# Adaptive max pooling on one core: from Tile's dependencies to one critical section with semaphores set by hand

## The chip, the core and the metric

The kernel runs on one core of a Trainium2 chip. The metric is the device time of one execution in microseconds (us), here the median of several runs. Beside it there is a profile of one further execution, taken by the hardware profiler: its span goes from the first to the last instruction of the program, and its times are counted from the start of that span.

Four parts of the core matter here. SP (SyncE) issues transfers (DMAs) and waits on semaphores. DVE (VectorE) reduces. ACT (ScalarE) issues one transfer. Sixteen DMA engines move the data for all of them. A transfer that is issued adds 16 to a semaphore when it has landed. "SPq" or "DVEq" in the profile is the part of an engine that handles waits and issues; these aren't counted as busy.

## The reference

The input is 32 x 256 x 4096 float32 (134.2 MB); each row of 4096 is cut into 256 windows, and the output has the maximum of each window (8.4 MB).

```python
for i in range(output_size):
    start = int(i * length / output_size)
    end = int((i + 1) * length / output_size)
    result[:, :, i] = np.max(x[:, :, start:end], axis=-1)
```

4096 / 256 = 16, so all windows are 16 long and don't overlap. In memory the task is a list of 32 x 256 x 256 windows, each of 16 neighbouring numbers.

## The kernel before, in words

**Layout.** The 2,097,152 windows are dealt to 128 partitions, 16384 each, in two groups. In group A each partition has 13436 neighbouring windows, in group B 2948. Every transfer is one contiguous run per partition.

**Loads.** Group A comes in 14 loads of 128, 12 times 1024, and 1020 windows per partition, from the end of the group to its start; group B in three, of 1024, 1024 and 900. That makes 17 loads. One of 1024 windows has 65536 bytes per partition, 8.4 MB in all. All are issued by SP, in the order of the loop: the small first one at L87, the 16 others at L96.

**Ring.** There are two places for loads in the tile `ring`, each 1024 + 152 windows wide. Loads take the two places in turn, and each second load of a place is shifted by 152 windows (`GAP`). DVE reduces a load in two pieces, 872 and 152 windows, and begins with the 872 windows that the next load of this place will overwrite. That next load needs the first piece only. It doesn't touch the other 152 windows.

**Reductions.** `pooled` (L56) is one `reduce_max` over the 16 numbers of each window, from `ring` to the tile `kept`, where all results but those of the last load stay. The last load is reduced in one piece, into the end of its own place in `ring`. There are 32 reductions: 1 + 15 x 2 + 1.

**Stores.** There are three: group A from `kept` (6718 KB), group B's first two loads from `kept` (1024 KB), and the last 900 windows from `ring` (450 KB). The last one is issued by ACT (L114), the other two by SP (L117). `tc.no_sync_barrier()` ahead of them keeps their place in the order of the program: they stand behind all loads in SP's stream and therefore in its DMA queue.

**Who makes the waits.** All of it is written in a Tile context. Tile follows which bytes of which tile each instruction reads and writes, and makes the semaphores and waits: a reduction waits for its load, a load for the landing of the older load in this place and for the first piece of its reduction, a store for its reductions. An instruction carries a wait of its own; where there are more, short EVENT_SEMAPHORE instructions stand ahead of it on the same engine. L134 is the program's opening (constants and a barrier of all engines), L148 the Tile context, to which its closing is put down: waits of SP for the transfers, a barrier of all engines, a clearing of the semaphores, and a second barrier.

Of the kernel before, what the change touches and what calls it, by code (L numbers as in the profile page):

```python
# [1 line left out]

# [4 lines left out]


@with_exitstack
def kernel(  # L10
    ctx: ExitStack,
    tc: tile.TileContext,
    x: bass.AP,
    output_size: bass.AP,
    out: bass.AP,
):

    nc = tc.nc
    P = nc.NUM_PARTITIONS
    fp32 = mybir.dt.float32

    B, C, L = x.shape
    O = int(output_size)  # L30
    assert L % O == 0, (L, O)
    W = L // O
    total = B * C * O // P
    assert B * C * O % P == 0

    CHUNK = 1024
    GAP = 152
    FIRST = 128
    LOADS_A, LOADS_B = 13, 2

    LESS = 4
    group_a = [FIRST] + [CHUNK] * (LOADS_A - 1) + [CHUNK - LESS]
    last = total - sum(group_a) - LOADS_B * CHUNK
    group_b = [CHUNK] * LOADS_B + [last]
    assert 0 < last and last * (W + 1) <= CHUNK * W

    pool = ctx.enter_context(tc.tile_pool(name="pool", bufs=1))
    ring = pool.tile([P, 2 * (CHUNK + GAP) * W], fp32, tag="ring", name="ring")
    kept = pool.tile([P, total - last], fp32, tag="kept", name="kept")

    xw = x.flatten_outer_dims().rearrange("r (o w) -> (r o) w", w=W)
    ow = out.flatten_outer_dims().rearrange("r o -> (r o)")

    def pooled(dst, at, n):

        nc.vector.reduce_max(  # L56
            out=dst,
            in_=ring[:, at * W : (at + n) * W].rearrange("p (n w) -> p n w", w=W),
            axis=mybir.AxisListType.X,
        )  # L60

    taken = 0

    def group(n):

        nonlocal taken
        span = slice(taken * P, (taken + n) * P)
        taken += n
        return (
            xw[span].rearrange("(p n) w -> p (n w)", p=P),  # L70
            ow[span].rearrange("(p n) -> p n", p=P),
        )

    stores = []
    n_loads = 0
    base = 0
    for g, loads in enumerate((group_a, group_b)):
        xg, og = group(sum(loads))
        a = sum(loads) if g == 0 else 0
        for n in loads:  # L80
            if g == 0:
                a -= n
            xn = xg[:, a * W : (a + n) * W]
            dst = kept[:, base + a : base + a + n] if n != last else None
            if n == FIRST:

                nc.sync.dma_start(  # L87
                    out=ring[:, CHUNK * W : (CHUNK + n) * W], in_=xn
                )
                pooled(dst, CHUNK, n)  # L90
            else:

                low = n_loads % 2 * (CHUNK + GAP)
                moved = n_loads // 2 % 2
                at = low + moved * GAP
                nc.sync.dma_start(out=ring[:, at * W : (at + n) * W], in_=xn)  # L96
                if n != last:
                    cut = CHUNK - GAP if moved else GAP
                    parts = [(0, cut), (cut, n)]
                    for u, v in parts if moved else parts[::-1]:  # L100
                        pooled(dst[:, u:v], at + u, v - u)
                else:
                    end = (at + CHUNK) * W
                    last_kept = ring[:, end - n : end]
                    pooled(last_kept, at, n)
                n_loads += 1
            if g:
                a += n
        full = a - last if g else sum(loads)
        stores.append((og[:, 0:full], kept[:, base : base + full]))  # L110
        base += full
    assert taken == total

    nc.scalar.dma_start(out=og[:, full : full + last], in_=last_kept)  # L114
    tc.no_sync_barrier()
    for dst, src in stores:
        nc.sync.dma_start(out=dst, in_=src)  # L117


# [1 line left out]
_INS = ['x', 'output_size']  # L121
_OUTS = [((32, 256, 256), 'float32')]

_NUMBERS = {'output_size': 256}


# [26 lines left out]
```

## Time and profile before

| what | value |
|---|---|
| median of 3 runs | 335.02 us (335.02 to 335.04) |
| span of the profiled execution | 333.1 us, 113 instructions |
| its own time: span, and what lies around it | 333.1 us, and 335.02 - 333.1 = 1.9 us if it took as long as the median |
| DVE busy | 276.5 us (83%), 32 reductions |
| of these: 872 windows, 14 times | 205.6 us, 14686 ns each |
| 152 windows, 15 times | 40.1 us, 2676 ns each |
| the last 900 windows | 15.1 us |
| moved | 134.22 MB read, 8.39 MB written, 428 GB/s over the span |
| issue to landing: load of 8192 KB | 24.0 us, median of 14 |
| big store, small store (SP) | 37.2 us, 18.1 us |
| last store (ACT) | 4.2 us |

The page's parts used below are: 2, the span in 40 slices with one digit of busy tenths each; 3, the DMA queues (q1 is fed by SP, q10 by ACT) with packets, megabytes, and the share of the 16 engines that they took; 6, the transfers from issue to landing. A timeline row gives start and length in us, engine, line, operation, tiles and shapes, how many instructions were merged in the row, and in brackets how long the engine sat idle before it and what ended that. A row of waits reads: who waited, for whom, us in total, how often, the longest. A transfer's time from issue to landing includes its time in the queue behind others.

### The profile page before, as it was taken

To read this page: it belongs to the slowest core of one execution; us is meant where nothing else is said; L and a number is where in the kernel's file an instruction comes from. 1 tells how busy PE (TensorE), PEld (TensorE's weight loads), DVE (VectorE), ACT (ScalarE), POOL (GpSimd) and SP (SyncE) were. 2 spreads that over 40 slices of the span, in tenths; PEclk is the share of its full clock that TensorE was granted. 3 is DMA by queue.
4 is the path that set the end of the run, shared out by engine and by line. 5 is a ranking of instruction groups with operands and counts; after the bars stand their busy time and mean duration, and the time that the engine had idled before them with its cause. 6 is when DMAs were issued, how large, how long until landed. Compare 5 with 4: busy or idle time off the path is not lost.

```text
span 333.1 us, 113 instructions
## 1 busy us (share of the span) xinstructions
DVE 276.5 (83%) x32; POOL 0.2 (0%) x4
## 2 busy tenths in 40 slices
DVE  2009979797997979799797979979797998979993
POOL 0000000000000000000000000000000000000000
DMA  9898989899898989899898989899898989899996
GB/s 378 378 504 378 504 378 496 386 441 441 378 504 378 504 378 496 386 457 425 378 504 378 504 378 504 378 441 441 385 494 377 504 378 504 378 458 443 421 413 285
DMA packets 2880, 142.61 MB, mean 428 GB/s; under 512 B 320, under 2 KB 320, under 8 KB 448
## 3 DMA queue, kind: packets, MB, share of 16 engines
q1 hardware_dynamic: 2736, 142.15, 98.8%
q10 hardware_dynamic: 144, 0.46, 0.3%
HBM read 134.22 MB, written 8.39 MB: 428 GB/s over the span
## 4 chain that ended last, share of the span: by engine, by line
DMA 57%; DVE 36%; DVEq 5%; issue 0%; SPq 0%
DMA ring<-in_x_dram 57%; DVE kept L56 36%; DVEq L148 5%; SPq L87 0%
## 5 line engine op out<-in xcount | busy, mean ns | idle before, releaser
L56 DVE TENSOR_REDUCE kept<-ring 128x152 f32<-128x2432 f32 (+3 forms) x31 | 261.4, 8472 | 51.5 <-DMA ring<-in_x_dram 51.5
L56 DVE TENSOR_REDUCE ring<-ring 128x900 f32<-128x14400 f32 x1 | 15.1, 15144 | 0.0
L134 POOL MEMSET const-bfloat16-1.0<- 128x1 bf16 x1 | 0.1, 102 | 0.0
L134 POOL MEMSET const-uint8-127<- 128x1 uint8 x1 | 0.1, 102 | 0.0
L134 POOL MEMSET const-float32-0.0<- 128x1 f32 x1 | 0.1, 99 | 0.2 <-issue 0.2
L134 POOL MEMSET const-float32-1.0<- 128x1 f32 x1 | 0.1, 99 | 0.0
## 6 DMA issues: line engine op xcount, KB each, us to landing
ring<-in_x_dram SPq DMA_DIRECT2D x1, 8160.0 KB, 23.9
ring<-in_x_dram SPq DMA_DIRECT2D x1, 7200.0 KB, 21.6
out_dram<-kept SPq DMA_DIRECT2D x1, 6718.0 KB, 37.2
ring<-in_x_dram SPq DMA_DIRECT2D x1, 1024.0 KB, 4.7
out_dram<-kept SPq DMA_DIRECT2D x1, 1024.0 KB, 18.1
out_dram<-ring ACTq DMA_DIRECT2D x1, 450.0 KB, 4.2
ring<-in_x_dram SPq DMA_DIRECT2D x14, 24.0
```

The costliest lines, as they stand in the source:

```text
L56: nc.vector.reduce_max(out=dst, in_=ring[:, at * W : (at + n) * W].rearrange("p (n w) -> p n w", w=W), axis=mybir.AxisListType.X,)
L134: nc = _bacc.Bacc("TRN2", target_bir_lowering=False, num_devices=1)
L148: with _tile.TileContext(nc) as tc:
```

## The change

The loop no longer issues anything. It makes a list, `plan`, with for each load its source, place, size, the load whose first piece it needs, the pieces and where they go. A second loop inside `tc.tile_critical()` issues the same instructions in the same order on the same engines, and every wait is written out: three semaphores for landings, used in turn, one that counts reductions, and one for each store. Inside such a section Tile makes no waits of its own; it treats the section as one unit. Each reduction adds 1 to `pooled`. At the end SP waits for the three stores. The barrier-like `tc.no_sync_barrier()` is gone.

The first loop, cut to its core:

```diff
-                nc.sync.dma_start(
-                    out=ring[:, CHUNK * W : (CHUNK + n) * W], in_=xn
-                )
-                pooled(dst, CHUNK, n)
+                at, moved, needs = CHUNK, 0, None
+                pieces = [(0, n)]
...
+                moved = n_full // 2 % 2
+                at = n_full % 2 * (CHUNK + GAP) + moved * GAP
+                needs = n_full - 2
+                cut = CHUNK - GAP if moved else GAP
+                pieces = [(0, cut), (cut, n)] if moved else [(cut, n), (0, cut)]
+                if n == last:
+                    pieces = [(0, n)]
+                n_full += 1
...
+            plan.append((xn, at, n, needs, pieces, dsts))
...
-    nc.scalar.dma_start(out=og[:, full : full + last], in_=last_kept)
-    tc.no_sync_barrier()
-    for dst, src in stores:
-        nc.sync.dma_start(out=dst, in_=src)
```

The section (`first_piece[k]` is the count of reductions at which the first piece of full load k is done, `all_pieces[i]` the count after all pieces of load i):

```diff
+    with tc.tile_critical():
+        for i, (xn, at, n, needs, pieces, dsts) in enumerate(plan):
+            if needs is not None and needs >= 0:
+                nc.sync.wait_ge(pooled, first_piece[needs])
+            nc.sync.dma_start(
+                out=ring[:, at * W : (at + n) * W], in_=xn
+            ).then_inc(landed[i % 3], 16)
+            nc.vector.wait_ge(landed[i % 3], 16 * (i // 3 + 1))
+            for (u, v), dst in zip(pieces, dsts):
+                nc.vector.reduce_max(
+                    out=dst,
+                    in_=ring[:, (at + u) * W : (at + v) * W].rearrange(
+                        "p (n w) -> p n w", w=W
+                    ),
+                    axis=mybir.AxisListType.X,
+                ).then_inc(pooled, 1)
+        for i, (dst, src) in enumerate(stores[:2]):
+            nc.sync.wait_ge(pooled, all_pieces[len(group_a) - 1 if i == 0 else -2])
+            nc.sync.dma_start(out=dst, in_=src).then_inc(stored[i], 16)
+        nc.scalar.wait_ge(pooled, all_pieces[-1])
+        nc.scalar.dma_start(out=stores[2][0], in_=stores[2][1]).then_inc(stored[2], 16)
+        for sem in stored:
+            nc.sync.wait_ge(sem, 16)
```

More of the change, by code (lines that the diff above doesn't have):

```diff
@@ L52 @@
     ow = out.flatten_outer_dims().rearrange("r o -> (r o)")
[L54 to L59, printed above, removed]
-        )
     taken = 0
@@ L72, in group @@
         )
+    plan = []
     stores = []
-    n_loads = 0
     base = 0
+    n_full = 0
     for g, loads in enumerate((group_a, group_b)):
@@ L83 @@
             xn = xg[:, a * W : (a + n) * W]
-            dst = kept[:, base + a : base + a + n] if n != last else None
             if n == FIRST:
-                nc.sync.dma_start(
-                    out=ring[:, CHUNK * W : (CHUNK + n) * W], in_=xn
-                )
-                pooled(dst, CHUNK, n)
-            else:
[L93 to L102, printed above, removed]
+                at, moved, needs = CHUNK, 0, None
+                pieces = [(0, n)]
+            else:
+                moved = n_full // 2 % 2
[6 more added lines that the diff above has]
+                n_full += 1
+            dsts = []
+            for u, v in pieces:
+                if n == last:
                     end = (at + CHUNK) * W
                     last_kept = ring[:, end - n : end]
-                    pooled(last_kept, at, n)
-                n_loads += 1
+                    dsts.append(last_kept)
+                else:
+                    dsts.append(kept[:, base + a + u : base + a + v])
+            plan.append((xn, at, n, needs, pieces, dsts))
             if g:
@@ L112 @@
     assert taken == total
-    nc.scalar.dma_start(out=og[:, full : full + last], in_=last_kept)
-    tc.no_sync_barrier()
-    for dst, src in stores:
-        nc.sync.dma_start(out=dst, in_=src)
+    stores.append((og[:, full : full + last], last_kept))
+    landed = [nc.alloc_semaphore(f"landed{i}") for i in range(3)]
+    pooled = nc.alloc_semaphore("pooled")
+    stored = [nc.alloc_semaphore(f"stored{i}") for i in range(3)]
+    count, first_piece, all_pieces = 0, [], []
+    for xn, at, n, needs, pieces, dsts in plan:
+        if needs is not None:
+            first_piece.append(count + 1)
+        count += len(pieces)
+        all_pieces.append(count)
+    with tc.tile_critical():
[21 more added lines that the diff above has]
+            nc.sync.wait_ge(sem, 16)
 _INS = ['x', 'output_size']
```

## The prediction

> **What bounds the kernel now.** I read the page from the transfers inwards: first the busy slices and the queues, then the waits, then the two ends.
>
> Part 2 of the page has one digit for each fortieth of the span, and part 3 the share of the 16 transfer engines that each queue took:
>
> ```profile
> DMA  9898989899898989899898989899898989899996
> ...
> q1 hardware_dynamic: 2736, 142.15, 98.8%
> q10 hardware_dynamic: 144, 0.46, 0.3%
> ```
>
> The queue that SP feeds (q1) occupies the 16 engines 98.8% of the whole span. The same view asked for the stretch 5 to 330 us, without the ends, says:
>
> ```profile
> DMA packets 2553, 140.09 MB, mean 431 GB/s; under 512 B 274, under 2 KB 274, under 8 KB 274
> ...
> q1 hardware_dynamic: 2553, 140.09, 99.6%
> ```
>
> So for 325 us there is no idle transfer time to win. The chain of waits seems to say otherwise: it gives DMA 57% and VectorE (DVE) 36%, in turn. The timeline and the waits of SP's queue show why that isn't a bound of DVE:
>
> ```profile
> 24.78 17.28 DVE L56 TENSOR_REDUCE kept<-ring 128x872 f32<-128x13952 f32 x2 [17.04 <-DMA ring<-in_x_dram]
> 39.50 19.68 SPq L96 DMA_DIRECT2D ring<-in_x_dram  x2
> 44.14 17.28 DVE L56 TENSOR_REDUCE kept<-ring 128x872 f32<-128x13952 f32 x2 [2.08 <-DMA ring<-in_x_dram]
> ```
>
> ```profile
> SPq L96 <- DVE kept L56: 205.6, 14, 14.7
> SPq L96 <- DMA ring<-in_x_dram: 78.4, 14, 22.7
> ```
>
> A load lands and DVE starts at 24.78. After its first piece (14.7 us, the wait of SP just above) SP issues the next load at 39.50; but the load issued before it is still moving and lands only at 44.14. The queue therefore holds at least 44.14 - 39.50 = 4.6 us of work whenever a load is issued. The chain follows the buffer that was released last; the queue in front of it is what takes the time. DVE idles about 2.07 us ahead of each load.
>
> At the end the question is whether the last reduction or the transfers are late:
>
> ```profile
> 312.82 15.14 DVE L56 TENSOR_REDUCE ring<-ring 128x900 f32<-128x14400 f32 x1
> 312.94 0.34 SPq L117 DMA_DIRECT2D out_dram<-kept  x1
> 328.00 0.37 ACTq L114 DMA_DIRECT2D out_dram<-ring  x1
> ```
>
> ACT issues the last store at 328.00, and its landing, 4.2 us later (part 6), is the last event of the work. The queue view of 328 to 330.2 us shows that it isn't DVE that sets this:
>
> ```profile
> q1 hardware_dynamic: 115, 0.92, 99.4%
> issues: line engine op xcount, KB each, median us to landing
> out_dram<-ring ACTq DMA_DIRECT2D x1, 450.0 KB, 4.2
> ```
>
> In these 2.2 us no packet of q10, the ACT queue, runs; all 16 engines are still at SP's last store (99.4%). The first load of the kernel shows how soon packets can follow an issue: it is issued at 0.73, and the stretch 0.5 to 1.5 has a DMA share of 0.00, the stretch 1.5 to 2.0 one of 0.94, so 0.8 to 1.3 us. ACT's packets could have run from about 329.0 (at 1.0). They start after 330.2, so ACT and the reduction ahead of it have some 1.2 us of room (0.9 with the longer start).
>
> So **the time is one stream of transfers, from the first issue at 0.73 to the landing at 332.2**, with what stands before and after it. An edit counts only if it moves the first issue, opens a hole in the stream, or changes what follows 332.2.
>
> **The base of the sum.** The profiled span is 333.1 us. The median of the plain runs is 335.02, so 335.02 - 333.1 = 1.9 us lie around the span. No edit touches what lies there, and I carry the 1.9 over.
>
> **The change, part by part.**
>
> Loads. Before each of 14 loads SP waits twice, for an older landing (78.4 us in all) and then for DVE (205.6 us); the new text has only the second wait, with the same piece as its condition. The landing wait always ends first (at 44.1, against a DVE piece that ends at 58.8), so taking it out saves 14 short instructions of 17 to 28 ns that nobody waits for: 0. The cover is the 4.6 us in the queue; without it each later issue would cost its own length.
>
> DVE's waits. They are now instructions ahead of the reductions. Today one such instruction stands on DVE at this line, 21 ns long; others are part of the reduction. 17 of them are 0.4 us of DVE time, at the most 0.1 us each if the reduction behind a wait starts later, 1.7 us, against 2.07 us of idle time ahead of each load. In the middle it costs nothing. At the end, two of them (load 16 and the last) delay the last reduction by 0.04 to 0.2 us, and ACT's own separate wait is 0.04 more (its one wait instruction today takes 38 ns). All of it lies inside the 1.2 us of room: 0. Without that room it would be 0.1 to 0.24 us.
>
> Stores. SP now waits for all of group A before the first store: those pieces end at 256.93 + 17.21 = 274.1, and the store is issued at 291.4, behind the last load. 0. The second store waits for the same piece as today (21.1 us of SP's time, until 312.9), while its queue still holds 6.7 MB of the first store: 0. What is queued behind this wait on SP is only the final waits. The order on q1 (loads, big store, small store) and on q10 stays.
>
> Entering the section. Tile opens and closes a section on all engines together, and the trace of before has no such boundary. Its nearest rows are the barriers of the closing code, as waits of SP on the last engine to arrive:
>
> ```profile
> SPq L148 <- DMA out_dram<-kept: 17.8, 1, 17.8
> SPq L148 <- DMA out_dram<-ring: 1.1, 1, 1.1
> SPq L134 <- PEq L134: 0.7, 1, 0.7
> SPq L148 <- PEq L148: 0.6, 2, 0.4
> ```
>
> The two closing barriers cost SP 0.6 us: 0.2 for the plain one, 0.4 for the one with drains and a clearing of semaphores in it; the opening one 0.7, with four memsets inside. A boundary at the entry stands ahead of the first issue, so its price is the price of the kernel. From below: SP leaves the opening barrier at about 0.66 and issues at 0.73, so no more than 0.07 can be gained. From above: 0.7, as the opening. I take 0.2, the plain barrier, because nothing has to be drained there.
>
> Leaving the section, and the tail. Today SP's wait for ACT's store (the 1.1 us row) ends at 332.2; one more wait of 28 ns and two drains stand before the closing barrier, until 332.4; the span ends at 333.1. In the new text the wait for ACT's store is the last of three, so the wait behind it goes: -0.1. The section's end adds a boundary: 0.2 by the same row. From below: if the section's own end stands in for the closing, at most the 333.1 - 332.2 = 0.9 us after the landing could go. From above: 0.7 again.
>
> The Trainium skill's page "Runtime: NRT & Kernel Launch", section "The ~15µs preamble/postamble breakdown", prices a pass over all five engines at about 355 ns (8 hops of 44). It speaks of the runtime's barrier, not of Tile's, and against this change: by it two boundaries would be 0.7 us, an estimate, and the kernel would come to 335.6. The trace's 0.2 decides for the sum above.
>
> Sum: 333.1 + 0.2 (entry) + 0.2 (exit) - 0.1 (wait) = 333.4 us of span, and 333.4 + 1.9 = **335.3 us**, 0.1% over before. Its own range is 335.0 to 335.6, each boundary between nothing and 0.35.
>
> **The rivals.**
>
> Slower: heavy boundaries. Each end of the section costs not a plain barrier but one with drains, 0.4 us, up to the 0.7 of the opening. For it: leaving a section has to make sure that every engine is done, as the closing code has. Against: at both places the engines have nothing left to do. 333.1 + 0.8 to 1.4 - 0.1 + 1.9 = 335.7 to 336.3. It is slower by over 0.2% (0.67 us) from 0.39 us for a boundary on. Chance 0.20.
>
> Faster: a shorter closing. Since all work lies in the section, the closing has no semaphores of loads and reductions to look after, and the barrier with the clearing (0.4) or nearly everything after the landing (0.9) falls away: 334.6 to 334.1. For it: four wait instructions of SP stand there for eight semaphores that Tile made itself. Against: three of the four are over before 332.2, and the barriers come with the Tile context, which stays. It decides from 0.67 us, three quarters of that stretch. Chance 0.12.
>
> Not what it says: Tile's closing waits stay as they are, and the three waits stand ahead of them; then nothing goes and 335.4 is the time, not to be told from no change. Chance 0.10.
>
> Slower by a hole: a hand-set count releases a load over 4.6 us late, each time, and the queue runs dry. Each further us then counts 14 times: from 0.05 us past that room on it decides (14 x 0.05 = 0.7), and with 0.1 it gives 335.3 + 1.4 = 336.7. Against: the counts name the same pieces as today. Chance 0.03.
>
> **How the numbers follow.** My forecast has 0.55. Within 0.2% of before, about what a measurement of this kernel can tell from no change, lie the forecast and the closing that stays: 0.65. Faster by more: 0.12. Slower by more: 0.20 + 0.03 = 0.23. The range is 334.6 to 336.2: it leaves out the shorter closing (0.12), the hole (0.03) and the dearest end of the heavy boundaries (some 0.04).
>
> **What would show it.** In the profile after, q1 should again hold 98 to 99% of the span, and loads should land 19.3 to 19.4 us apart. The first issue should come at 0.9 instead of 0.73, the last landing at 332.4, and 0.9 to 1.0 us should follow it. If the first issue stays at 0.73, there is no barrier at the entry. If more than 1.6 us follow the landing, the heavy boundaries are right; if less than 0.5, the shorter closing. The forecast is wrong in its ground if a zero appears among the DMA digits, or if ACT's packets start at once after its issue: then the last reduction counts, and the waits on DVE with it.

## The result, and the profile after

| | before | after |
|---|---|---|
| median of 21 runs each | 335.09 us (334.92 to 335.37) | 335.66 us (335.52 to 335.82) |
| ratio, 95% interval | | 1.0017 (1.0012 to 1.0023) |
| span of the profiled execution | 333.1 us | 334.0 us |

The changed kernel takes 0.57 us (0.17%) longer. 335.3 was forecast, 0.28 us over before; the sign is right and the size about half.

The stream of transfers is as it was. The page's queue rows of the profile after:

```profile
DMA  9898989989898989899898989899998989899996
...
q1 hardware_dynamic: 2736, 142.15, 98.6%
q10 hardware_dynamic: 144, 0.46, 0.3%
```

The two waits ahead of a load have become one, and the sum is about the same: 284.8 us where there were 205.6 + 78.4 = 284.0. Here are SP's waits after:

```profile
SPq L127 <- DVE kept L132: 284.8, 14, 37.6
SPq L141 <- DVE kept L132: 21.1, 1, 21.1
SPq L145 <- DMA out_dram<-ring: 18.9, 1, 18.9
...
SPq L176 <- PEq L176: 0.5, 2, 0.3
```

The loss stands at the two ends. The chain in order of time (start, length, what) begins like this, first before, then after:

```profile
0.66 0.07 issue
0.73 0.37 SPq L87
```

```profile
0.71 0.01 SPq L123
0.72 0.06 issue
0.78 0.03 SPq L176
0.81 0.12 issue
0.94 0.38 SPq L127
```

L123 is the section, L176 the Tile context. SP sends a signal, waits for its own signal in a branch (DVE and ACT do so too, PE and POOL have no such instruction), and 0.12 us pass until the first issue after the branch. The first load is issued at 0.94 instead of 0.73: 0.21 us.

The other end is the code of the section after the last landing, in the view of one line from 332.7 us on (engine, operation, count, shortest, median and longest duration in ns, first and last start):

```profile
L123 SPq EVENT_SEMAPHORE  x2: 17/22/28, 333.0 to 333.2; - x2
L123 SPq COMPARE_BRANCH  x1: 33/33/33, 332.8 to 332.8; - x1
L123 ACTq DRAIN  x1: 8/8/8, 333.0 to 333.0; - x1
L123 DVEq DRAIN  x1: 10/10/10, 333.0 to 333.0; - x1
L123 SPq DRAIN  x1: 7/7/7, 333.1 to 333.1; - x1
L123 SPq NOP  x1: 13/13/13, 333.2 to 333.2; - x1
```

ACT's store is issued at 328.55 and lands 4.2 us later, at 332.73 by the trace. Then come a branch, a signal to three engines, a drain on each, and SP's waits for the answers; only at 333.3 does the closing of the Tile context begin. No instruction here lasts over 33 ns; the time passes between them, behind SP's branch, as at the entry, and in the handing over between engines. From the last landing to the end of the span it is 333.97 - 332.73 = 1.24 us, before it was 333.06 - 332.20 = 0.86: 0.38 us. In e4, e8 and e5 below, which have the same end, it is 1.24, 1.24 and 1.22 us.

0.21 + 0.38 = 0.59 us, against 0.57 measured. The two profiled spans are 0.9 us apart, because the stream between the ends took 331.5 us in one execution and 331.8 in the other. The medians of the spans say that those 0.3 us are the scatter of single executions: they are 333.3 to 333.4 for the kernel before (its runs beside e1, e5 and e9) and 333.9 for the changed one. Less the ends of the profiles, 0.73 + 0.86 and 0.94 + 1.24, both leave a stream of 331.7 to 331.8 us.

### The profile page after: what moved, and what is told of

It reads as the page before. It is cut to its first block, busy times and chain, and to the rows that moved or that the text cites. A ratio compares the mean times of both kernels' runs of the same rounds, so it can differ in the third digit from the quotient of the medians.

```text
span 334.0 us, 105 instructions
## 1 busy us (share of the span) xinstructions
DVE 276.5 (83%) x32; POOL 0.2 (0%) x4
## 3 DMA queue, kind: packets, MB, share of 16 engines
q1 hardware_dynamic: 2736, 142.15, 98.6%
## 4 chain that ended last, share of the span: by engine, by line
DMA 57%; DVE 40%; issue 0%; SPq 0%
DMA ring<-in_x_dram 57%; DVE kept L132 36%; DVE ring L132 5%; SPq L127 0%; SPq L176 0%; SPq L123 0%
```

## The experiments

The theory was that the whole loss is made by the two ends of the section, and that the waits set by hand, the counters and the order of work cost and gain nothing. Its rival was that the hand-set waits slow the stream. Further runs test what the prediction leaned on: the cover of 4.6 us ahead of each load, and the room of ACT's store. "Around the span" is a run's time less its span.

**e1: the same waits, no section.**

```diff
-    nc = tc.nc
+    nc = tc
...
-    pool = ctx.enter_context(tc.tile_pool(name="pool", bufs=1))
-    ring = pool.tile([P, 2 * (CHUNK + GAP) * W], fp32, tag="ring", name="ring")
-    kept = pool.tile([P, total - last], fp32, tag="kept", name="kept")
+    ring = nc.alloc_sbuf_tensor("ring", [P, 2 * (CHUNK + GAP) * W], fp32).ap()
+    kept = nc.alloc_sbuf_tensor("kept", [P, total - last], fp32).ap()
...
-    with tc.tile_critical():
+    if True:
...
-    with _tile.TileContext(nc) as tc:
-        tile_adaptive_max_pool_1d_kernel(tc, *args)
+    tile_adaptive_max_pool_1d_kernel(nc, *args)
```

> The same loads, reductions, stores and hand-set waits as in the changed kernel, but with no section and no Tile context around them: nothing is entered or left, and SP's three waits for the stores are the last instructions. Theory 1 (the section's two ends are the whole loss: 0.21 us at the entry and 0.38 us after the last landing): the first issue is back at 0.73 us, the stream of transfers lasts 331.5 us as before, and with the closing (0.8 us after the landing) gone as well the time is 335.09 - 0.8 = 334.3 us, at least below 334.7. Rival (the waits set by hand slow the stream itself; in the two profiles first issue to last landing is 331.5 us before and 331.8 after): the stream stays at 331.8 and the time is 334.6 us. Second rival (the closing is needed anyway, the runtime's own ending takes its place): 335.1 us, as before.

Measured: 333.94 us, ratio 0.9965 (0.9952 to 0.9977) to before. The chain begins as it did before the change, and behind SP's waits for the stores (L144) no further instruction follows:

```profile
0.73 0.37 SPq L126
```

```profile
L144 SPq EVENT_SEMAPHORE  x2: 17/22/28, 331.4 to 332.6; - x2
```

The first issue is back at 0.73 with all waits set by hand, so the waits don't move it. The time fell by 1.7 us against the changed kernel and is 0.4 us under what the theory said: the medians of the spans are 333.4 and 332.6, so 0.8 us went in the span, as expected, and another 0.4 around it (1.35 instead of 1.8). The second rival's 335.1 is refuted. The time alone doesn't refute the first rival, whose 334.6 didn't reckon with the 0.4 us either, and the profiled run does have a stream of 331.8 us. The median span does: less 0.73 and the 0.05 us behind the landing it leaves 331.8 us, against the 331.7 to 331.8 of before and after. The 331.5 was one short execution. e9 asks where the other 0.4 us went.

**e9: e1 with one barrier at the end.**

```diff
         for sem in stored:
             nc.sync.wait_ge(sem, 16)
+        nc.all_engine_barrier()
```

> The kernel of e1 (no section, no Tile context) with one plain barrier of all engines after SP's waits for the stores. In e1 the span got 0.75 us shorter than before's (332.55 against 333.3, medians of its runs) and what lies around it 0.45 us (1.35 against 1.8). Theory (the second part comes from the engines that end early and do their share of the runtime's ending while SP still waits; a barrier takes that away): span 332.55 + 0.2, around it 1.8, time 334.55 us. Rival (the time around the span is shorter because nothing of Tile is left in the program, barrier or not): 332.75 + 1.35 = 334.1 us.

Measured: 334.59 us (0.9986 of before, 0.9977 to 0.9995), the median of the spans 332.8, so 1.8 us around it. SP's wait in the barrier:

```profile
SPq L145 <- PEq L145: 0.2, 1, 0.2
```

The barrier costs 0.2 us inside the span and 0.45 outside. The rival's 334.1 is refuted, and the time fits the theory: without the barrier, the four other engines come to the end of the program early, and their part of what the runtime does after a kernel no longer stands behind SP's. That it is this part is inferred from the times; the views show no instruction of it. The Trainium skill, page "Runtime: NRT & Kernel Launch", section "The ~15µs preamble/postamble breakdown", lists after a kernel a barrier that waits for all engines, about 1.5 us, and then a reset of some 51 semaphores for each engine, about 1.5 us. No run here shows either; what it is that can be done early stays open, and the runs only put it at 0.45 us. (Against the before measured beside each, e1 gains 1.21 and e9 0.46 us, so the whole barrier is worth 0.65 to 0.75 us.)

**e2: a section in the kernel before.**

```diff
+    idle = nc.alloc_semaphore("idle")
+    with tc.tile_critical():
+        for eng in (nc.vector, nc.scalar, nc.sync):
+            eng.nop().then_inc(idle, 1)
```

> The kernel before with one section ahead of everything, in which DVE, ACT and SP do one empty instruction each; all waits of the loads, reductions and stores are still Tile's. Theory 1 (the ends of a section cost 0.2 us to enter and 0.4 us to leave, and all of it ahead of the first issue counts in full): first issue at 1.3 us instead of 0.73, and 335.09 + 0.6 = 335.7 us. Rival (the loss comes from the waits set by hand): 335.1 us, and the first issue at most 0.2 us later.

Measured: 338.17 us, 3.0 us more than before, which neither theory gives. The chain shows what happened:

```profile
0.79 4.85 DMA ring<-in_x_dram
5.63 0.02 issue
5.65 0.02 SPq L153
...
6.03 0.07 issue
6.10 21.99 DMA ring<-in_x_dram
```

Tile put the first load ahead of the section's work and made the section wait for its landing. The second load is issued at 6.10 instead of 1.15, and from about 5.3 to 7.0 us no transfer runs in the trace. As a price of the ends the run is worthless; it shows what else a section can do in a stream of Tile's instructions.

**e5: the same section ahead of the changed kernel's own,** where no transfer can slip in front.

> The changed kernel with a second section, of one empty instruction each on DVE, ACT and SP, ahead of the first, so that no transfer can slip in between. Theory 1 (entering costs SP 0.2 us, leaving 0.5 us of which 0.1 stood in the closing anyway, and all that lies ahead of the first issue counts): first issue at 0.94 + 0.7 = 1.6 us, time 335.66 + 0.7 = 336.4 us, landing to end as in the changed kernel (1.2 us). Rival (what was lost comes from the hand-set waits in the section, not from its ends): 335.7 us.

Measured: 336.35 us (1.0039 of before, 1.0026 to 1.0052), 0.69 us more than with one section. The chain:

```profile
1.51 0.03 SPq L180
1.55 0.12 issue
1.67 0.38 SPq L131
```

The first issue moved by 1.67 - 0.94 = 0.73 us, and the time by 0.69. The theory held: one section, entered and left, costs 0.7 us, and whatever stands ahead of the first issue counts in full.

**e4 and e8: a later last reduction.** e4 adds the reduction shown, e8 one of 2432 numbers.

```diff
+    spare = pool.tile([P, 40], fp32, tag="spare", name="spare")
...
+            if n == last:
+                back = plan[i - 1][1] * W
+                nc.vector.reduce_max(
+                    out=spare,
+                    in_=ring[:, back : back + 640].rearrange("p (n w) -> p n w", w=16),
+                    axis=mybir.AxisListType.X,
+                )
             nc.vector.wait_ge(landed[i % 3], 16 * (i // 3 + 1))
```

> The changed kernel with one more reduction of 640 numbers per partition ahead of the last one, by the rate of the others (14.69 us for 13952 numbers) 0.7 us; its result is not used. Theory (ACT's store has some 1.1 us of room, since its packets wait for SP's last store): ACT issues 0.7 us later, its packets start at the same time, 335.66 us. Rival (the last reduction sets the end): 336.3 us.

> The changed kernel with one more reduction of 2432 numbers per partition ahead of the last one (2.6 us by the 152-window row), its result unused. Theory (ACT's store has 1.1 us of room): ACT issues at 331.1 instead of 328.5, 2.6 - 1.1 = 1.5 us of it show, 337.2 us, and ACT's packets start about 1 us after the issue. Rival (no room, DVE sets the end): 335.66 + 2.6 = 338.2 us. Rival (ACT's store needs its 2.1 us from issue to the first packet by itself): also 338.2, with the packets 2.1 us after the issue.

Measured: e4 335.65 us, against 335.66 of the changed kernel, though ACT issues at 329.28 instead of 328.55. e8 336.65 us, 0.99 more. The timeline and the stretches of e8 (start and end; share of the transfer engines in the last but one column, then GB/s):

```profile
331.12 0.37 ACTq L152 DMA_DIRECT2D out_dram<-ring  x1
```

```profile
331.00:331.50 0.50, 0.09 (x1) 0.00 (x0) 1.00 0.00 0
331.50:332.00 0.50, 0.00 (x0) 0.00 (x0) 1.00 0.02 7
332.00:332.50 0.50, 0.00 (x0) 0.00 (x0) 1.00 1.02 410
```

Here SP's store is over, nothing stands ahead of ACT's, and its packets run 0.9 us after the issue; it lands after 2.5 us instead of 4.2. So the other 1.7 us of the 4.2 were time behind SP's store. ACT was 331.12 - 328.55 = 2.57 us later, the end 0.99: the room is 1.6 us, and what DVE's separate waits may add, 0.2 us at most, stays inside it. The Trainium skill, page "DMA: Bandwidth & Descriptors", section "Specifications", gives about 0.6 us to the first byte for transfers from SP and ACT; this trace has 0.9, and the room follows from the trace.

**e3, e6 and e7: loads issued later.** e3 lets a load wait for both pieces; e6 and e7 cut the second piece and let it wait for 40 or 76 windows more. The edit of e6:

```diff
-                pieces = [(0, cut), (cut, n)] if moved else [(cut, n), (0, cut)]
+                pieces = [(0, cut), (cut, cut + 40), (cut + 40, n)] if moved else [(cut, n), (0, 40), (40, cut)]
...
-            first_piece.append(count + 1)
+            first_piece.append(count + min(2, len(pieces)))
```

> The changed kernel with each load waiting for both pieces of the reduction in its place, not for the first alone: each of 13 loads is issued 2.6 us later. Theory (the queue holds 4.6 us of work at each issue, so the wait is covered): 335.66 us, within 0.2, and still 16 busy transfer engines. Rival (the chain of waits is right: loads and reductions wait for each other in turn, so each delay counts): 7 pairs in the chain times 2.6 us = 18 us more, 354 us.

> The changed kernel with the second piece cut in two (40 and 112 windows) and each load waiting for the first piece and these 40 windows: each of 13 to 14 loads is issued 0.7 us later, 3.9 us ahead of the landing before it in place of 4.6. Theory A (a queue with enough work in it: there is a threshold, which 0.7 us does not reach): 335.7 us, landings still 19.35 us apart. Theory B (the chain with a fixed 24.0 us from issue to landing: any delay counts once for each pair of loads): 7 x 0.7 = 4.9 us more, 340.5 us.

> The same with 76 and 76 windows: each load is issued 1.3 us later, 3.3 us ahead of the landing before it. Theory A: 335.7 us if 3.3 us of work are enough; the run with 2.0 us left lost 18 us (1.3 us a load), so a threshold between 2.0 and 3.3 gives 335.7, one above 3.3 at most 335.7 + 13 x 0.3 = 339 us. Theory B: 7 x 1.3 = 9 us more, 344.7 us.

Measured: e3 353.65 us (1.0559, 1.0524 to 1.0593), e6 339.5 (1.0123, 1.0086 to 1.016; single runs from 337.1 to 340.7), e7 345.49 (1.0298, 1.0277 to 1.0319). The cover that I had counted as 4.6 us isn't there: 0.7 us of it already costs 1.4 to 5.0 us. Nor is theory B right, though its sums are near in all three. The profiled execution of e6, a span of 334.9 us, in its timeline:

```profile
44.59 17.34 DVE L132 TENSOR_REDUCE kept<-ring 128x872 f32<-128x13952 f32 x3 [2.03 <-DMA ring<-in_x_dram]
...
63.94 17.34 DVE L132 TENSOR_REDUCE kept<-ring 128x872 f32<-128x13952 f32 x3 [2.02 <-DMA ring<-in_x_dram]
83.29 14.69 DVE L132 TENSOR_REDUCE kept<-ring 128x872 f32<-128x13952 f32 x1 [2.01 <-DMA ring<-in_x_dram]
```

The landings are 19.35 us apart in this stretch, with issues 0.7 us later, so issue to landing is 23.3 us here and not the fixed 24.0 of theory B. Further on in the same execution, the fastest of the four, they are up to 19.7 us apart, and the extra adds up to 1.0 us. In e7 loads go either way. Here are three issues of SP, and the reductions, each of which begins when a load has landed:

```profile
60.77 0.33 SPq L127 DMA_DIRECT2D ring<-in_x_dram  x1
80.12 0.33 SPq L127 DMA_DIRECT2D ring<-in_x_dram  x1
100.44 0.33 SPq L127 DMA_DIRECT2D ring<-in_x_dram  x1
```

```profile
64.08 17.34 DVE L132 TENSOR_REDUCE kept<-ring 128x872 f32<-128x13952 f32 x3 [2.02 <-DMA ring<-in_x_dram]
84.40 17.34 DVE L132 TENSOR_REDUCE kept<-ring 128x872 f32<-128x13952 f32 x3 [2.98 <-DMA ring<-in_x_dram]
103.75 17.34 DVE L132 TENSOR_REDUCE kept<-ring 128x872 f32<-128x13952 f32 x3 [2.02 <-DMA ring<-in_x_dram]
125.37 14.69 DVE L132 TENSOR_REDUCE kept<-ring 128x872 f32<-128x13952 f32 x1 [4.28 <-DMA ring<-in_x_dram]
```

The distances are 20.32, 19.35 and 21.62. The first and the third of these loads were issued 3.3 us ahead of the landing before them (64.08 - 60.77 and 103.75 - 100.44) and lose 1.0 and 2.3 us. The second was issued 84.40 - 80.12 = 4.3 us ahead and loses nothing: a load that lands late gives the next one more lead. All four loads of this execution that were issued 4.3 us ahead or more lose nothing, those at 3.3 to 3.7 lose between nothing and 2.3 us; in e6 loads at 3.9 to 4.2 lose up to 0.3 us, and in e3 single ones at 4.6 and 4.9 still lose 0.3. So there is a threshold, as in theory A, but a soft one, around 4 us, and not below 3.3. That late loads give back lead is probably also why theory B, with one loss for each pair, comes near. Where in the transfer path the threshold sits, these runs don't tell.

The busy digits hide such a loss. The page of e3, 18 us slower, has no zero among them:

```profile
DMA  9989999998998998989999898999998999989994
...
q1 hardware_dynamic: 2736, 142.15, 96.1%
```

96.1% of 352.0 us are 338 us of busy engines for the same 2736 packets; after it was 98.6% of 334.0, 329 us. Half of the loss is idle time, the other half is counted as busy, in packets of which some take longer. In e6 and e7 some 0.4 us more lie around the span (2.2 us); that isn't explained either.

**e10: issued earlier.** 960 windows a load, a shift of 216, 18 loads, otherwise e1.

```diff
-    CHUNK = 1024
-    GAP = 152
+    CHUNK = 960
+    GAP = 216
-    LOADS_A, LOADS_B = 13, 2
+    LOADS_A, LOADS_B = 14, 2
```

> The kernel of e1 with loads of 960 windows and a shift of 216 in the same ring (18 loads in place of 17). By the rows of the reductions and loads a load is then issued 5.6 us ahead of the landing before it (2 x 18.1 - 12.5 - 18.1) in place of 4.6. Theory (from 4.6 us on the engines lose nothing, the stream is at its floor): 333.94 us, within 0.2. Rival (the loss that showed at 3.9 us is still there in part at 4.6 us): up to 0.2 us a load, 3 us less, 331 us.

Measured: 333.89 us (0.9964 of before, 0.995 to 0.9977), beside 333.94 of e1. A load is issued at 36.36 and the one before it lands at 41.92, so 5.6 us lie between, and it gains nothing. At 4.6 us the stream is at its floor; the kernel stands just on the safe side of the threshold, and neither the change nor e1 moves it (39.88 to 44.52 after, 4.64 us). e1 and e10 beat the kernel before by 0.35% and the changed one by 0.5%.

## Why the prediction was right, and where it was off

- **The stream sets the time: right.** The first issue moved by 0.21 us in the change and by 0.73 more in e5, and the time followed. q1's share and the distance of the landings hardly changed.
- **Loads' waits, stores, increments at nothing: right.** e1 has all of them and none of the ends, and its first issue and the lead of its loads are those of before.
- **DVE's and ACT's waits inside ACT's room: right.** The room is 1.6 us; 1.2 was forecast, since I took 1.0 us from issue to packets where e8 shows 0.9, and let the packets start at 330.2, where they were still held up.
- **The entry: right in size, not in kind.** 0.2 was taken from a plain barrier, 0.21 came. But it isn't a barrier of all engines, as the prediction had it; it is a signal and a branch on SP, and the same branch on DVE and ACT.
- **The exit: the term that was mis-sized.** The sum had 0.2 for the boundary less 0.1 for a wait that goes, 0.1 in all; it measured 0.38. Leaving is a branch, a signal, a drain on each of three engines and two waits for their answers, all behind the last landing, and the closing comes after it. This one end had the price (about 0.5 with the wait that went) of the rival with heavy boundaries. That rival was priced with both ends heavy; a light entry with a heavy exit wasn't among the cases. With 0.38 in its place the sum is 335.02 + 0.59 = 335.6. The 335.66 lies just above the sum's own range, 335.0 to 335.6. Of the 0.36 us between 335.3 and 335.66, 0.28 are this term and 0.07 the base, 335.02 against a later 335.09. The 335.6 that stands in the prediction beside the sum comes nearer by luck: it has two equal ends of 0.35, and the trace has 0.21 and about 0.5.
- **"What would show it":** a first issue at 0.9 came (0.94); 0.9 to 1.0 us behind the landing didn't (1.24), and this is where the miss could be read. The sign for heavy boundaries, over 1.6 us, didn't come either, but it was set too high: by that rival's own prices 0.9 - 0.1 + 0.4 to 0.7, so 1.2 to 1.5 us, would follow the landing.
- **The shorter closing: it didn't come.** The Tile context closes nearly as before whatever is in the section: SP's two waits in it take 0.5 us instead of 0.6. The gain is real only where the context itself goes (e1).
- **The 4.6 us of cover: wrong as a number,** without harm here. I read the time between an issue and the landing before it as room. Of those 4.6 us less than 0.7 are free, so the rival with a hole would have begun long before "over 4.6 us late". And it needs no zero among the DMA digits, as e3 shows: the zero was no safe sign.

## What to carry to other kernels

Where one stream of transfers sets the time, price a change by the first issue and by what follows the last landing, and count there every signal that one engine has to wait for: a section cost 0.2 us to enter and 0.4 to leave, some four times what SP's own instructions in it last (46 ns to enter, 98 to leave). Replacing a framework's waits by hand is worth nothing while they lie beside the stream; the gain is in the closing that can be left out, 1.2 us here (the clearing of the semaphores goes with it). A queue that never runs dry, and transfer engines that look busy throughout, say nothing on how late the next transfer may be issued: try it with a small delay.

## What was not expected of the hardware

- A load of this kernel has to be issued some 4 us ahead of the end of the one before it: 4.6 and 5.6 us lose nothing, at 3.9 single runs lose 1.4 to 5 us in all, at 3.3 some loads lose 1 to 2.3 us each, at 2.0 the kernel loses 18 us. From issue to the first packet it is only 0.9 us on a free queue.
- Half of what is lost so doesn't appear as idle time: in e3 the same packets keep the engines busy for 338 us instead of 329.
- A barrier of all engines at the very end costs 0.65 to 0.75 us, of which the span shows 0.2.
